# Moving the key tiles' transposes, the gate products, the context shift rows and one pair's modulation in a two-layer diffusion block on one Trainium2 core

## The chip, the core and the metric

The kernel runs on one core of a Trainium2 chip. A core has a matrix engine (TensorE, PE in the profile), a vector engine (DVE), a scalar engine (ACT), a general engine (POOL) and a queue engine (SP) that mostly issues DMAs; each takes its own instructions in order, and semaphores tie them together. The metric is the device time of one execution in microseconds (us), here the median of three runs.

## The reference

Two layers of one backbone, over 1024 latent tokens and 256 context tokens, width 1024. Each layer is an adaLN-modulated, pre-normed mixer with a SiLU gate path and a residual. Layer 0 is grouped-query attention (16 query heads, 4 key heads), layer 1 is multi-head latent attention with compressed keys and values. Cut to what this change touches:

```python
def adaln_params(cond, w_mod, b_mod):
    return jnp.split(jax.nn.silu(cond) @ w_mod + b_mod, 3, axis=-1)      # shift, scale, gate

def kv_heads(kv_a, k_r, n):                                               # layer 1
    kv = (rms_norm(kv_a, p["kv_a_norm"]) @ p["w_kv_b"]).reshape(B, n, 16, 64 + 64)
    k_nope, v = jnp.split(kv, [64], axis=-1)
    return rms_norm(k_nope, p["k_nope_norm"]), rms_norm(k_r, p["k_rope_norm"]), v

def hybrid_layer(x, ctx, c, c_ctx, w_mod, b_mod, norm_w, mixer, ..., with_ctx_out):
    shift, scale, gate = adaln_params(c, w_mod, b_mod)
    shift_c, scale_c, gate_c = adaln_params(c_ctx, w_mod, b_mod)
    h = rms_norm(x, norm_w) * (1.0 + scale[:, None, :]) + shift[:, None, :]
    hc = rms_norm(ctx, norm_w) * (1.0 + scale_c) + shift_c
    y, yc = mixer(h, hc, ...)
    x = x + gate[:, None, :] * y                                          # ctx likewise, in layer 0 only
```

Layer 1's gate row, `silu(c) @ w_mod[:, 2048:] + b`, is needed only where layer 1's output projection is added to x, at the very end.

## The kernel before, in words

Every product of float32 values is made of three matmuls (`mm3`, lines L120, L121, L122): high part by high, high by low, low by high. Weights come by SP into raw buffers `wraw` (pool `rawp`, three buffers), are cast by ACT (`wa`, L184), and their low part is the difference, made by DVE or POOL (`wb`, L163). The stages follow one another: layer 0's projections (0 to 335 us), attention 0 (340 to 703), layer 0's output projection (704 to 831), layer 1's key stage (832 to some 940), its query stage (to 1105), attention 1 (1130 to 1542), layer 1's output projection (to the end).

Attention. A unit is a pair of heads; PE computes scores twice, once for the maxima (`mx`, reduced by DVE at L454 for layer 1 and L495 for layer 0's context units), once for the exponentials (`st`, ACT at L607, result `p`), and then multiplies `p` by v (`av`, `avt`). POOL adds up the `p` of a unit (`acp`, L640); DVE forms the sums (`squares`, `sums`, L705 to L707), and a row of reciprocals goes out and comes back as `rb`; POOL multiplies (`rb`, `os`, L739 and L740) and SP stores to `od`. The maxima become a row of shifts: `do_shift` turns the tile `top` into `turned`, and two DMAs put two rows of it into the tile `shift` (L521) or, for a context unit, `shift_ctx`. In attention 0 units 4, 9, 18 and 19 are context units. Where attention runs (`running`), ACT issues these DMAs, else SP. `Attention.run` takes pairs (t, end) of unit and half; behind a unit's squares it takes the next piece of weight preparation (`extra`, `parts`).

Output projection, `out_proj`. For each of ten tiles of 128 tokens (eight latent, two context): fetch the attention's rows (`oraw`), split them (`oh` by ACT at L870, `ol` by DVE at L871), 48 matmuls `y`, multiply by the gate row `gb` (`yt`, L888), add to `xt` (L889), then call `sink`. In layer 0 `sink0` stores `xt`, norms it (L307), and hands pairs of tiles to `modulate`, where 16 transposes (`tp`, L319) bring the pair into column form, DVE scales it (`hmod`, L323), and the halves `hh`, `hl` are made. A list `hold` delays a pair: `flush(1)` does the oldest pair held.

Key stage of layer 1. `staged(items, *stages)` runs a software pipeline: in step t, stage j is applied to item t - j, and `later` is a stage that does nothing. The stages are `kv_compress` (24 matmuls `mm` of 288 columns, then the norm: `kvms` L1677, `kvrs` by POOL L1680, `kvn` by DVE L1682 and L1683, and a rotary step that ends in L1694, on POOL from the third tile on), `kv_latent` (transposes `tp` of `kvn`, L1701 and L1702, split into `kvh`, `kvl`), `kv_expand` (12 matmuls `mmk` for keys and 12 `mmv` for values, `sq` L1729, `kss` L1731, `kn_ms` L144, `kn` L1714, `v` L1736) and `kv_store` (transposes of `kn`, L1750, `th` and `tl` at L1754 and L1755). DVE keeps the order in which the program writes its work there; PE's order is the scheduler's.

Gate products. `gate_cols(k)` loads 128 rows of w_mod's gate part (tile `wcols`, 512 KB, a `wraw` buffer), and `mod_cols` (L265) has DVE multiply it by the row u and sum: one SCALAR_TENSOR_TENSOR of 128x1024 per k, eight in all. After the eighth, `mod_cols_end` adds the bias (`top`, L271), turns it into a row (`turned`) and SP stores it to `gated`, from which `out_proj` of layer 1 loads `gb`. Here this stands in the key stage:

```python
        with in_order(mybir.EngineType.DVE):
            staged(range(TT), kv_compress, kv_latent, later_with_cols, later, kv_expand, store_all_but_last)
```

## Time and profile before

| | us |
|---|---|
| median of 3 runs | 1639.27 |
| the runs | 1636.88 to 1641.38 |
| the profiled execution's own time | 1638.23 |
| its span, first to last instruction | 1636.3 |
| PE busy | 1596.0 |
| DVE busy | 1150.5 |
| POOL busy | 961.7 |
| ACT busy | 641.2 |
| mean granted clock of PE | 0.995 |

A timeline row reads: start, duration, engine, line, operation, output <- inputs, shapes, count of instructions that the row joins, and in brackets how long the engine sat idle before it and what ended that. PE's matmuls overlap, so a matmul of 512 columns that shows 0.39 us takes a slot of about 0.23. ACTq and SPq are the queues' own instructions, above all the issue of DMAs; they hold the engine's later instructions while they last.

### The profile page before, as it was taken

How to read it: one execution, taken by the hardware profiler on the slowest of the kernel's cores; microseconds unless marked ns; L12 is line 12 of the kernel's file. 1: busy time of each engine (PE TensorE's matmuls, PEld its weight loads, DVE VectorE, ACT ScalarE, POOL GpSimd, SP SyncE). 2: the span in 40 equal slices, each digit the busy share in tenths (PEclk: the TensorE clock that was granted, in tenths of full speed). 3: DMA queues.
4: the chain of work that ended last, by engine and by line, in shares of the span. 5: the costliest groups of instructions: out<-in, count | busy, mean ns of one | idle time of the engine just before them, and what ended most of it. 6: DMA issues, size and time to landing. Idle time of an engine off the chain costs nothing.

```text
span 1636.3 us, 26486 instructions
## 1 busy us (share of the span) xinstructions
PE 1596.0 (98%) x9788; PEld 1178.3 (72%) x9788; DVE 1150.5 (70%) x1951; ACT 641.2 (39%) x943; POOL 961.7 (59%) x629
## 2 busy tenths in 40 slices
PE   7999999999999999999989999999999999999998
PEld 5776788865554555577878798987776767767587
DVE  2674876679998988746576767755778888788231
ACT  3652321235654555522244543341444544435310
POOL 2673640138999999923245555450768878777521
PEclk9999999999999999999999999999999999999999
DMA  8636566742533342274246867768456565562451
GB/s 285 213 106 192 170 196 231 215 134 56 130 82 98 94 108 78 71 224 152 96 138 182 239 200 201 221 202 197 114 137 154 124 149 117 136 145 70 131 179 64
DMA packets 215325, 246.77 MB, mean 151 GB/s; under 512 B 19802, under 2 KB 157266, under 8 KB 215196
## 3 DMA queue, kind: packets, MB, share of 16 engines
q1 hardware_dynamic: 214228, 244.83, 53.7%
q8 instruction: 77, 1.26, 0.3%
q14 instruction: 52, 0.43, 0.1%
q10 hardware_dynamic: 968, 0.25, 0.1%
HBM read 171.23 MB, written 73.63 MB: 150 GB/s over the span
## 4 chain that ended last, share of the span: by engine, by line
PE 84%; DMA 5%; DVE 4%; POOL 2%; ACT 2%; issue 2%; SPq 1%; DVEq 0%; POOLq 0%; ACTq 0%
PE st L600 21%; PE avt L654 9%; PE av L654 9%; PE mm L120 8%; PE mm L122 8%; PE mm L121 8%; PE mx L452 4%; PE y L120 3%; PE y L121 3%; PE y L122 3%; PE mx L486 2%; DVE wb L163 1%; DMA q1l<-tl 1%; PE mx L462 1%; DMA mraw<-in_l_w_mod 1%
## 5 line engine op out<-in xcount | busy, mean ns | idle before, releaser
L640 POOL TENSOR_TENSOR acp<-acp,p 128x1024 f32<-128x1024 f32 x188 | 448.6, 2386 | 12.6
L607 ACT ACTIVATE p<-st 128x1024 f32<-128x1024 f32 x328 | 336.3, 1027 | 154.5 <-PE st L600 145.7
L454 DVE TENSOR_REDUCE m<-mx 128x1 f32<-128x512 f32 x256 | 175.8, 691 | 66.2 <-PE mx L452 60.3
L640 POOL TENSOR_TENSOR acp<-p 128x1024 f32<-128x1024 f32 x34 | 81.5, 2398 | 191.7 <-ACT p L607 191.7
L495 DVE TENSOR_REDUCE m<-mx 128x1 f32<-128x1024 f32 x128 | 150.2, 1219 | 39.4 <-PE mx L486 38.9
L654 PE MATMUL avt<-p,v 128*64 128x512 f32 x672 | 149.3, 596 | 0.7 <-ACT p L607 0.6
L654 PE MATMUL av<-p,v 128*64 128x512 f32 x640 | 141.1, 595 | 0.0
L163 POOL TENSOR_TENSOR wb<-wraw,wa 128x512 fp32r<-128x512 f32 (+3 forms) x65 | 91.0, 1415 | 80.4 <-ACT wa L184 80.4
L120 PE MATMUL mm<-wa,hh 128*128 128x512 f32 (+2 forms) x336 | 126.1, 375 | 1.7 <-ACT hh L1041 1.1
L600 PE MATMUL st<-QH,KH 64*128 64x512 f32 x320 | 122.5, 407 | 0.6 <-DVE gth L354 0.5
L122 PE MATMUL mm<-wa,hl 128*128 128x512 f32 (+2 forms) x336 | 121.5, 362 | 1.6 <-DVE hl L1044 1.6
L121 PE MATMUL mm<-wb,hh 128*128 128x512 f32 (+2 forms) x336 | 121.1, 360 | 0.0
L600 PE MATMUL st<-QH,KL 64*128 64x512 f32 x320 | 117.9, 391 | 0.0
L600 PE MATMUL st<-QL,KH 64*128 64x512 f32 x320 | 117.6, 390 | 0.0
L654 PEld LDWEIGHTS avt<-p,v 128*64 128x64 f32 x672 | 46.0, 137 | 93.8 <-issue 82.9
L654 PEld LDWEIGHTS av<-p,v 128*64 128x64 f32 x640 | 44.3, 137 | 87.9 <-issue 87.3
L120 PE MATMUL mm<-hh,wa 128*128 128x512 f32 (+1 forms) x264 | 103.0, 390 | 0.9 <-ACT th L102 0.9
L120 PE MATMUL y<-wa,oh 128*128 128x512 f32 (+1 forms) x268 | 103.3, 386 | 0.0
L122 PE MATMUL y<-wa,ol 128*128 128x512 f32 (+1 forms) x268 | 102.8, 384 | 0.0
L121 PE MATMUL y<-wb,oh 128*128 128x512 f32 (+1 forms) x268 | 102.8, 384 | 0.0
L122 PE MATMUL mm<-hh,wb 128*128 128x512 f32 (+1 forms) x264 | 101.3, 384 | 0.0
L121 PE MATMUL mm<-hl,wa 128*128 128x512 f32 (+1 forms) x264 | 101.3, 384 | 0.0
(267 smaller groups left out, 4045.1 us busy)
## 6 DMA issues: line engine op xcount, KB each, us to landing
wraw<-in_l_w_in SPq DMA_DIRECT2D x28, 512.0 KB
wcols<-in_l_w_mod_t SPq DMA_DIRECT2D x24, 512.0 KB
KH<-k1h SPq DMA_DIRECT2D x32, 320.0 KB
KL<-k1l SPq DMA_DIRECT2D x32, 320.0 KB
rb<-rrow SPq DMA_DIRECT2D x72, 128.0 KB
mraw<-in_l_w_mod SPq DMA_DIRECT2D x16, 512.0 KB
wraw<-in_l_w_out SPq DMA_DIRECT2D x16, 512.0 KB
QA<-q0h SPq DMA_DIRECT2D x32, 256.0 KB
```

Of the source, the lines that this page charges most:

```text
L120: pe.matmul(ps, lhsT=lh(k), rhs=rh(k), start=first and i == 0, stop=False)
L121: pe.matmul(ps, lhsT=lh(k), rhs=rl(k), start=False, stop=False)
L122: pe.matmul(ps, lhsT=ll(k), rhs=rh(k), start=False, stop=last and i == len(ks) - 1)
L163: eng.tensor_sub(lo, a, b)
L452: pe.matmul(held["m"][:, cs], lhsT=q[:, t * P:(t + 1) * P], rhs=k[:, ks], start=j == 0, stop=j == len(pairs) - 1)
L454: dve.reduce_max(s["m"][:, i, n:n + 1], held["m"], axis=AX.X)
L486: pe.matmul(m[:, n * 512:n * 512 + 512], lhsT=q[:, i * P:(i + 1) * P], rhs=k[:, n * 512:n * 512 + 512], start=True, stop=True)
L495: dve.reduce_max(s["m"][:, i, 0:1], m, axis=AX.X)
L600: pe.matmul(ps[:, n * 512:(n + 1) * 512], lhsT=lh, rhs=rh, start=j == 0, stop=j == last)
L607: act.activation(p, ps, AF.Exp, scale=self.ops["scale"])
L640: pool.tensor_add(t, a, b)
L654: pe.matmul(s["av"][64 * n:64 * n + 64, :], lhsT=s["v"][:, kt, u["vc"]:u["vc"] + 64], rhs=p[:, n * 512:(n + 1) * 512], start=kt == kts[0], ...
```

## The change

Four things, independent of each other.

First, `sink0` calls `flush(1)` for tile 3 and no longer for tile 2. The first pair's modulation so comes behind the products of tile 3, the fourth tile; the later pairs stay where they are. Second, the context units' two shift DMAs are issued by SP also while attention runs. Third, in the key stage one `later` moves ahead of `kv_latent`: a tile's transposes are made two steps behind its products, and its expansion at the step at which it was. Fourth, the gate products leave the key stage. Attention gets a table `beside` that maps (unit, half) to a function; it loads the first two pieces at unit 10, does one product each at units 11, 12 and 13, two at 14, and three and the end of the row at (15, 0). The row u is loaded there, and piece k + 2 is fetched behind product k.

```diff
--- before.py
+++ after.py
@@ -373,6 +373,7 @@
             self.started = 0
             self.done = 0
             self.todo = []
+            self.beside = {}
             self.last_lat = [u for u in units if u["kind"] == "lat"][-1]
 
         def open_early(self, st):
@@ -518,7 +519,7 @@
                 r = turned[at_:at_ + 32, :]
                 turn_squares(r, raw(m))
                 for n in range(2):
-                    (act if self.running else sp).dma_start(raw(s["crow"][n]), r[4 * n:4 * n + 4, :])
+                    (act if self.running and u["kind"] == "lat" else sp).dma_start(raw(s["crow"][n]), r[4 * n:4 * n + 4, :])
 
             self.turns.append((self.units.index(u), turn))
 
@@ -815,6 +816,7 @@
                             if late:
                                 self.add_up(u, [], [])
                             self.squares(u, p2s[n1 // 2:])
+                        self.beside.get((t, int(end)), lambda: None)()
                         if t % 2 and end:
                             if parts:
                                 parts()
@@ -1619,9 +1621,9 @@
                 sp.dma_start(x1d[tt * P:(tt + 1) * P, :], xt)
             norm_rows(xt, small)
             xs_of.setdefault(tt // 2, []).append(xt)
-            if tt % 2 == 0:
+            if tt % 2 == 0 and tt != 2 or tt == 3:
                 flush(1)
-            else:
+            if tt % 2:
                 hold.append((tt // 2, xs_of[tt // 2]))
 
         def started0():
@@ -1758,26 +1760,11 @@
 
         kept = []
 
-        u = st.enter_context(tc.tile_pool(name="urow1", bufs=1, **right)).tile([P, D], F32, name="u0", tag="u0")
-        sp.dma_start(u, ud[0:1, :].broadcast_to([P, D]))
-
-        def gate_cols(k):
-            w = rawp.tile([P, D], F32, name="wcols", tag="wraw")
-            sp.dma_start(w, ins["l1_w_mod_t"][2 * D + k * P:2 * D + (k + 1) * P, :])
-            mod_cols(w, u.unsqueeze(1), w, 2, k, (0,))
-            if k == KT - 1:
-                mod_cols_end(2)
-
         def store_all_but_last(tt, held):
             kept.append(held) if tt == TT - 1 else kv_store(tt, held)
 
-        def later_with_cols(tt, kv):
-            if tt < KT:
-                gate_cols(tt)
-            return kv
-
         with in_order(mybir.EngineType.DVE):
-            staged(range(TT), kv_compress, kv_latent, later_with_cols, later, kv_expand, store_all_but_last)
+            staged(range(TT), kv_compress, later, kv_latent, later, kv_expand, store_all_but_last)
         wqa = load_weight(w_in1, KT, 288, 384)
         with tc.manual_schedule(engines={mybir.EngineType.PE, mybir.EngineType.DVE}):
             early[0] = proj1(0, wqa, 384)
@@ -2018,6 +2005,26 @@
     stL, stLP = ExitStack(), ExitStack()
     at.open_late(stL, stLP)
     first = []
+    u = stE.enter_context(tc.tile_pool(name="urow1", bufs=1, **right)).tile([P, D], F32, name="u0", tag="u0")
+    sp.dma_start(u, ud[0:1, :].broadcast_to([P, D]))
+    cols = {}
+
+    def gate_fetch(k):
+        cols[k] = rawp.tile([P, D], F32, name="wcols", tag="wraw")
+        sp.dma_start(cols[k], ins["l1_w_mod_t"][2 * D + k * P:2 * D + (k + 1) * P, :])
+
+    def gate_cols(n):
+        for _ in range(n):
+            k = cols.pop("next", 0)
+            mod_cols(cols[k], u.unsqueeze(1), cols[k], 2, k, (0,))
+            cols["next"] = k + 1
+            if k + 2 < KT:
+                gate_fetch(k + 2)
+            if k == KT - 1:
+                mod_cols_end(2)
+
+    at.beside = {(10, 1): lambda: [gate_fetch(k) for k in range(2)], (11, 1): lambda: gate_cols(1), (12, 1): lambda: gate_cols(1),
+                 (13, 1): lambda: gate_cols(1), (14, 1): lambda: gate_cols(2), (15, 0): lambda: gate_cols(3)}
     at.run(24, 2, pieces, lambda: first.extend(fetch_first(1, 3)))
     stLP.close()
     stE.close()
```

Line numbers of the new kernel are one or two higher from `do_shift` on (L521 is L522, L675 is L676, L1701 is L1703, L871 is L873), and 13 lower behind the key stage.

PE in layer 0's output projection, at the first pair's transposes. The names carry buffer numbers: y_7343 is the second half of tile 2, xt_7162 and xt_7167 are tiles 0 and 1. Before:

```order
L120 MATMUL y_7343<-wa_3339,oh_7339 128x512
L121 MATMUL y_7343<-wb_3340,oh_7339 128x512
L122 MATMUL y_7343<-wa_3339,ol_7340 128x512
L319 MATMUL tp_7410<-ident_72,xt_7162 128x128
L319 MATMUL tp_7410<-ident_72,xt_7167 128x128
```

The same transposes in the new kernel, where y_7414 is the second half of tile 3:

```order
L120 MATMUL y_7414<-wa_3339,oh_7410 128x512
L121 MATMUL y_7414<-wb_3340,oh_7410 128x512
L122 MATMUL y_7414<-wa_3339,ol_7411 128x512
L319 MATMUL tp_7483<-ident_72,xt_7162 128x128
L319 MATMUL tp_7483<-ident_72,xt_7167 128x128
```

The transposes moved behind 48 more products; the second pair's follow after the 48 of tile 4.

DVE at the same place, before (L307 norms a tile, L323 scales the transposed pair, L888 and L889 are the sum of the next tile):

```order
L307 TENSOR_SCALAR xt<-xt,x_rs 128x1024
L144 TENSOR_SCALAR x_ms<-xss 128x1
L888 TENSOR_TENSOR yt<-y,gb 128x512
L307 TENSOR_SCALAR xt<-xt,x_rs 128x1024
L888 TENSOR_TENSOR yt<-y,gb 128x512
L323 TENSOR_SCALAR hmod<-tp,A_114,B_116 128x256
L889 TENSOR_TENSOR xt<-xt,yt 128x512
L323 TENSOR_SCALAR hmod<-tp,A_114,B_116 128x256 x3
L144 TENSOR_SCALAR x_ms<-xss 128x1
L323 TENSOR_SCALAR hmod<-tp,A_114,B_116 128x256 x2
```

And in the new kernel:

```order
L307 TENSOR_SCALAR xt<-xt,x_rs 128x1024
L144 TENSOR_SCALAR x_ms<-xss 128x1
L890 TENSOR_TENSOR yt<-y,gb 128x512
L307 TENSOR_SCALAR xt<-xt,x_rs 128x1024
L890 TENSOR_TENSOR yt<-y,gb 128x512
L891 TENSOR_TENSOR xt<-xt,yt 128x512
L873 TENSOR_TENSOR ol<-oraw,oh 128x1024
L144 TENSOR_SCALAR x_ms<-xss 128x1
L307 TENSOR_SCALAR xt<-xt,x_rs 128x1024
L890 TENSOR_TENSOR yt<-y,gb 128x512 x2
L323 TENSOR_SCALAR hmod<-tp,A_114,B_116 128x256
L891 TENSOR_TENSOR xt<-xt,yt 128x512
```

DVE's first work on the pair moved behind tile 3's split and sum.

PE at the head of the key stage, from the first tile's expansion on, before:

```order
L120 MATMUL mmk<-wa,kvh 128x512
L121 MATMUL mmk<-wb,kvh 128x512
L1702 MATMUL tp<-ident,kvn 32x128
L122 MATMUL mmk<-wa,kvl 128x512
L120 MATMUL mmk<-wa,kvh 128x512
L121 MATMUL mmk<-wb,kvh 128x512
L122 MATMUL mmk<-wa,kvl 128x512
L1701 MATMUL tp<-ident,kvn 128x128 x2
L120 MATMUL mmv<-wa,kvh 128x512
L121 MATMUL mmv<-wb,kvh 128x512
L1702 MATMUL tp<-ident,kvn 32x128
L122 MATMUL mmv<-wa,kvl 128x512
```

And in the new kernel:

```order
L120 MATMUL mmk<-wa,kvh 128x512
L121 MATMUL mmk<-wb,kvh 128x512
L1704 MATMUL tp<-ident,kvn 32x128
L1703 MATMUL tp<-ident,kvn 128x128 x2
L120 MATMUL mmv<-wa,kvh 128x512
L121 MATMUL mmv<-wb,kvh 128x512
L1704 MATMUL tp<-ident,kvn 32x128
L122 MATMUL mmk<-wa,kvl 128x512
L120 MATMUL mmk<-wa,kvh 128x512
L121 MATMUL mmk<-wb,kvh 128x512
L122 MATMUL mmk<-wa,kvl 128x512
L122 MATMUL mmv<-wa,kvl 128x512
```

The transposes of the third tile (the second L1701 row's place) stand behind two products here and behind six before, and a fourth tile's, which stood among the products further on, come a step later.

DVE at the tail of the key stage, before:

```order
L103 TENSOR_TENSOR krl<-tp,krh 32x128
L265 SCALAR_TENSOR_TENSOR wcols,cols_71<-wcols,u_8241 128x1024
L163 TENSOR_TENSOR wb<-wraw,wa 128x384
L271 TENSOR_TENSOR top_84<-cols_71,colsT 128x8
L95 STREAM_TRANSPOSE turned<-top_84 32x32 x4
L1731 TENSOR_REDUCE kss<-sq 128x8
L144 TENSOR_SCALAR kn_ms<-kss 128x8
L1731 TENSOR_REDUCE kss<-sq 128x8
L144 TENSOR_SCALAR kn_ms<-kss 128x8
L1714 TENSOR_TENSOR kn<-mmk,kn_rs 128x512 x2
```

And in the new kernel:

```order
L103 TENSOR_TENSOR krl<-tp,krh 32x128
L1733 TENSOR_REDUCE kss<-sq 128x8
L163 TENSOR_TENSOR wb<-wraw,wa 128x384
L144 TENSOR_SCALAR kn_ms<-kss 128x8
L163 TENSOR_TENSOR wb<-wraw,wa 128x384
L1733 TENSOR_REDUCE kss<-sq 128x8
L144 TENSOR_SCALAR kn_ms<-kss 128x8
L1716 TENSOR_TENSOR kn<-mmk,kn_rs 128x512 x2
```

The last gate product, the sum `top` and its turn are gone from between `krl` and `kss`, and three weight parts `wb` stand elsewhere.

DVE at the end of attention 1, before:

```order
L707 RECIPROCAL turned<-turned 32x32
L99 TENSOR_REDUCE squares<-p 128x64
L99 TENSOR_REDUCE squares<-acp 128x32
L95 STREAM_TRANSPOSE sums<-squares 32x96 x4
L705 TENSOR_REDUCE turned<-sums 32x32
L706 TENSOR_REDUCE turned<-turned 32x32
L707 RECIPROCAL turned<-turned 32x32
L871 TENSOR_TENSOR ol<-oraw,oh 128x896 x3
```

And in the new kernel:

```order
L708 RECIPROCAL turned<-turned 32x32
L99 TENSOR_REDUCE squares<-p 128x64
L265 SCALAR_TENSOR_TENSOR wcols,cols_71<-wcols,u_11903 128x1024 x2
L99 TENSOR_REDUCE squares<-acp 128x32
L95 STREAM_TRANSPOSE sums<-squares 32x96 x4
L706 TENSOR_REDUCE turned<-sums 32x32
L707 TENSOR_REDUCE turned<-turned 32x32
L708 RECIPROCAL turned<-turned 32x32
L265 SCALAR_TENSOR_TENSOR wcols,cols_71<-wcols,u_11903 128x1024 x3
L271 TENSOR_TENSOR top_84<-cols_71,colsT 128x8
L95 STREAM_TRANSPOSE turned<-top_84 32x32 x4
L873 TENSOR_TENSOR ol<-oraw,oh 128x896 x3
```

Two products stand ahead of the last squares but one, and three products with the row's end between the last reciprocal and layer 1's first `ol`.

## The prediction

> **What bounds the kernel now.** I read the page's busy times first, then the chain of waits of TensorE (PE), then the timeline around each wait that the change touches, then the other engines' timelines there.
>
> ```profile
> PE 1596.0 (98%) x9788; PEld 1178.3 (72%) x9788; DVE 1150.5 (70%) x1951; ACT 641.2 (39%) x943; POOL 961.7 (59%) x629
> ```
>
> PE is busy for 1596.0 of 1636.3 us, and the change neither adds nor removes a matmul. What it can win lies in the 40 us of idle PE time, and in time at a lower clock. The view of waits (engine, line waited for: us in total, times, longest) lists that idle time; four of its rows belong to places that the change touches.
>
> ```profile
> PE tp L1701 <- DVE kvn L1682: 3.7, 3, 1.3
> ...
> PE mmk L120 <- DVE kn L1714: 2.3, 2, 1.5
> PE tp L319 <- DVE xt L307: 2.2, 1, 2.2
> ...
> PE mx L486 <- DVE m L495: 1.9, 2, 1.4
> ```
>
> **Part 1: the first pair's transposes behind tile four.** In layer 0's output projection the 16 transposes L319 of tiles 0 and 1 stand right behind the products y of tile 2. Timeline of PE, then DVE, then windows (busy time of PE, its weight load, DVE, ACT, POOL; third from the right is the granted PE clock), then PE at a later pair:
>
> ```profile
> 736.66 0.39 PE L122 MATMUL y<-wa,ol 128*128 128x512 f32 x1
> 737.34 0.30 PE L319 MATMUL tp<-ident,xt 128*128 128x128 f32 x1 [0.29 <-DVE x_ms L144]
> 739.80 2.81 PE L319 MATMUL tp<-ident,xt 128*128 128x128 f32 x15 [2.16 <-DVE xt L307]
> ...
> 744.27 0.39 PE L122 MATMUL y<-wa,ol 128*128 128x512 f32 x1
> ```
> ```profile
> 738.44 1.30 DVE L307 TENSOR_SCALAR xt<-xt,x_rs 128x1024 f32<-128x1024 f32 x1 [0.58 <-DMA x1d<-xt]
> ```
> ```profile
> 742.00:743.00 1.00, 1.00 (x5) 0.90 (x4) 1.00 (x4) 1.00 (x3) 0.00 (x0) 0.50 0.00 0
> ...
> 766.00:777.00 11.00, 11.00 (x54) 9.20 (x53) 8.98 (x15) 3.43 (x6) 4.81 (x4) 1.00 0.56 183
> 777.00:788.00 11.00, 11.00 (x50) 9.11 (x49) 4.12 (x6) 2.21 (x3) 1.84 (x2) 1.00 0.28 89
> ```
> ```profile
> 812.03 1.91 PE L319 MATMUL tp<-ident,xt 128*128 128x128 f32 x16
> 813.70 0.48 PE L120 MATMUL y<-wa,oh 128*128 128x512 f32 x1
> ```
>
> The second row stops because tile 1 is normed only at 738.44 to 739.74. Behind the wait of 2.16 us the clock is 0.50. From the slot after the last y (736.66 + 0.23 = 736.89) to the start of the sixth y of tile 3 (744.27) go 7.38 us. A later pair needs 813.70 - 812.03 = 1.67 us for its 16 transposes, and the first five y need about 0.31 + 4 x 0.23 = 1.22: 2.89. So 4.5 us are lost here, 2.45 of them waits and 2.0 the low clock. With tile 3's products (48 x 0.23 = 10.9 us) ahead of the transposes, both tiles have been normed for some 8 us when PE gets there. I take the whole 4.5. What is late next: pair 1 follows one tile later instead of two, so DVE gets two heavy tiles in a row. The windows of 11 us show DVE at 8.98 in a tile with a pair and 4.12 in one without; 8.98 twice still fits. Bounds: 2.5 (the low clock comes anyway) to 4.5.
>
> The Trainium skill, "TensorE: Matmul & The Clock Gate", part on HAM oscillation, says that PE idle for more than about 3.4 us brings the half rate. The idle time here is 2.45 us in all, and the half clock came nonetheless; read literally, the page would not lay it to this wait, and the sum would be 2.0 smaller. I go by the trace.
>
> **Part 2: context rows by SyncE (SP).** The context unit's two shift DMAs leave ACT's queue. ACT, DVE and PE in attention 0, at the second context unit:
>
> ```profile
> 495.83 0.58 ACTq L521 DMA_DIRECT2D shift<-turned  x1
> 496.98 2.38 ACTq L521 DMA_DIRECT2D shift_ctx<-turned  x2
> 499.40 1.14 ACT L184 CAST wa<-wraw 128x512 fp32r<-128x512 f32 x2 [8.68 <-DMA sg<-sgd]
> 500.45 0.58 ACT L675 COPY os<-avt 128x512 f32<-128x512 f32 x1
> ```
> ```profile
> 500.57 1.86 DVE L163 TENSOR_TENSOR wb<-wraw,wa 128x512 fp32r<-128x512 f32 x1 [2.41 <-ACT wa L184]
> ```
> ```profile
> 501.08 0.50 PE L600 MATMUL st<-QA,KA 64*128 64x512 f32 x2 [1.08 <-ACT os L675]
> ...
> 503.62 0.50 PE L486 MATMUL mx<-KA,QA 64*128 64x512 f32 x2 [1.35 <-DVE m L495]
> ```
>
> ACT cannot cast wa before its two issues are through at 499.36; os follows, PE waits 1.08 for it, and wb, held up by wa, keeps DVE from the maxima, for which PE waits 1.35. Without the two, wa starts right behind the lane shift (about 496.5), three us earlier, and both waits close: 2.4 us. On SP the two issues (2.4 us there too at worst) stand between loads of QA and QL for a later unit, which hides them. At the other context units nothing waits for ACT: nothing. Bounds: 0 (the lane shift's own wait, until 495.83, sets it) to 2.4; I take 2.4, since ACT's rows join without a gap.
>
> **Part 3: key tiles two steps behind.** Head of the key stage, PE, then POOL and DVE:
>
> ```profile
> 849.78 0.41 PE L1701 MATMUL tp<-ident,kvn 128*128 128x128 f32 x2 [1.19 <-DVE kvn L1682]
> ...
> 852.02 0.28 PE L1702 MATMUL tp<-ident,kvn 128*32 128x128 f32 x1 [1.37 <-POOL kvn L1694]
> ...
> 853.91 0.50 PE L120 MATMUL mmk<-wa,kvh 128*128 128x512 f32 x1 [0.68 <-ACT v L1736]
> ...
> 857.98 0.40 PE L120 MATMUL mm<-wa,hh 128*128 128x288 f32 x1 [0.68 <-ACT v L1736]
> ...
> 863.89 0.47 PE L120 MATMUL mmv<-wa,kvh 128*128 128x512 f32 x1 [0.76 <-ACT sq L1729]
> ```
> ```profile
> 850.56 1.41 POOL L1694 TENSOR_TENSOR kvn<-krt,krt 128x32 f32<-128x32 f32 x1
> ```
> ```profile
> 850.65 1.20 DVE L265 SCALAR_TENSOR_TENSOR wcols<-wcols,u 128x1024 f32<-128x1024 f32 x1
> ```
>
> The first two of the three waits for kvn (3.7 - 1.19 = 2.5 us) stay: the order of PE is the same up to there. The five waits shown sum to 4.68. The third tile's transposes are still early (in the new order only two products stand before them, so they wait again, about 1.2). The wait for POOL falls from 1.37 to about 0.5, since the gate product beside which L1694 took 1.41 is gone; the two for the copies of v stay; the last (0.76) goes, since the fourth tile's transposes now come a whole step later. That is 0.9 + 0.8 and some 0.3 for matmuls that restart less often: 2.0. Bounds: 0 (the waits only move) to 4.7.
>
> **Part 4: gate products at the attention's end.** Two places. Where they leave, the tail of the key stage (PE; DVE; POOL; ahead of it the two waits for kn L1714, 2.3 us):
>
> ```profile
> 911.96 0.50 PE L120 MATMUL mmv<-wa,kvh 128*128 128x512 f32 x1 [0.99 <-ACT v L1736]
> ```
> ```profile
> 907.53 1.84 DVE L265 SCALAR_TENSOR_TENSOR wcols<-wcols,u 128x1024 f32<-128x1024 f32 x1
> ...
> 909.96 0.86 DVE L95 STREAM_TRANSPOSE turned<-top 32x32 f32<-32x32 f32 x4
> ```
> ```profile
> 905.91 2.38 POOL L163 TENSOR_TENSOR wb<-wraw,wa 128x384 fp32r<-128x384 f32 x2
> ```
>
> The last product (1.84) and the turn of the row (0.86) stand on DVE ahead of the sums that kn waits for, and eight loads of 512 KB stand ahead of the next weights. 1.84 + 0.86 = 2.7 us earlier on DVE against 0.99 + 2.3 = 3.3 of waits: I take 2.5, bounds 1 to 3.3. In between, the stage is bound by PE, and seven products that leave there give nothing.
>
> Where they arrive, units 11 to 15 of attention 1. DVE, POOL, SP and PE:
>
> ```profile
> 1496.38 1.39 DVE L454 TENSOR_REDUCE m<-mx 128x1 f32<-128x512 f32 x2 [2.02 <-PE mx L452]
> ...
> 1523.46 0.35 DVE L707 RECIPROCAL turned<-turned 32x32 f32<-32x32 f32 x1
> 1540.35 3.77 DVE L871 TENSOR_TENSOR ol<-oraw,oh 128x896 fp32r<-128x896 f32 x3 [16.54 <-ACT oh L870]
> ```
> ```profile
> 1484.83 9.73 POOL L640 TENSOR_TENSOR acp<-acp,p 128x1024 f32<-128x1024 f32 x4
> ...
> 1528.86 9.72 POOL L640 TENSOR_TENSOR acp<-acp,p 128x1024 f32<-128x1024 f32 x4
> ```
> ```profile
> 1532.04 1.75 SPq L839 DMA_DIRECT2D oraw<-od  x3
> ```
> ```profile
> 1544.24 0.50 PE L108 MATMUL y<-wa,oh 128*128 128x512 f32 x1
> ```
>
> One product of 1.20 us falls into DVE's gap of 2.02 before a unit's maxima, when POOL's adds are over (1484.83 + 9.73 = 1494.56): free. Once the last unit's maxima are taken nothing of PE waits for DVE, and behind the last reciprocal (1523.81) it idles 16.54 us, long enough for the last three and the row's turn. But the 1.84 shows what POOL does to such a product: POOL's wb ends at 908.29, 0.76 after the product was due, and 1.20 + 0.76 = 1.96 is close to 1.84. Beside the adds from 1528.86 on (2.43 each) three products and three adds alternate: the products end not three times 1.20 after about 1524 but near 1535, the store of the gated row follows at about 1536, and on SP the loads of oraw, which stood at 1532.04, come behind it, near 1539. The 12.2 us from that issue to the first y at 1544.24 hold a landing, a cast on ACT and the split ol (3.77 for three, 1.26 for one); with 7 of them gone, 5.2 are left, about what these need, so the first y may wait about 1 us. POOL's last adds end some 3.7 us later, which lies within the bounds. I take a loss of 0.8; bounds 0 to 4. The eight fetches go on SP behind the next units' keys, and all but the last land a unit before their product; SP's queue waits for nothing else there that PE sees, so I cost them at nothing.
>
> The Trainium skill, "SBUF — State Buffer", section "SBUF: two separate sides", calls the ports shared by VectorE and GpSimd an exclusive lock for a whole instruction, also where VectorE has two inputs in SBUF. The rows 1.84 and 1.41 agree. Without such a lock, Part 4's loss would be 0.
>
> **Sum.** 4.5 + 2.4 + 2.0 + 2.5 - 0.8 = 10.6 us. The profiled execution took 1638.23 (span 1636.3 and 1.9 around it), so it would take 1627.6. It stood 1.04 below the median of the three runs, 1639.27; against that median 1628.7.
>
> **Rivals.**
> First, the key stage's waits only move (parts 3 and 4 give 0.5 in place of 4.5): 1632.7. For it: the copies of v and the third tile stay late. Against: DVE has 8 x 1.20 + 0.86 = 10.5 us less work there. 0.17.
> Second, the pair behind tile four brings its own wait: DVE at 8.98 of 11 for two tiles running, or the low clock was not the wait's doing. It costs 2 to 3: 1631.2, or 1630.7 where only the 2.0 of the clock stay. For it: the clock was 0.50 behind a mere 2.45 us of idle time. Against: DVE stays under 11, and the clock was 1.00 at the later pair, which did not wait. 0.13. The case of 1630.7 is also what the Trainium skill's page "TensorE: Matmul & The Clock Gate" (HAM oscillation) would give.
> Third, the rows' move does nothing, because ACT is held by the wait of the lane shift or SP puts the loads off: 1631.1. 0.12.
> Fourth, on the other side: DVE gets no turn between POOL's adds until POOL pauses, at 1538.58 or, with the unit's two multiplications, about 1541 (my estimate). Then three products and the turn (3.6 + 0.86) take until 1543 to 1546, and the gated store holds SP until then; oraw comes as now some 3 us later, and the first y another 8 to 12.2 behind it: at 1554 to 1561, 10 to 17 late. About 14 us lost where 11.4 are won: 1641.9. It decides from a gated store later than about 1544. Against: at 907.53 DVE did get its turn between two wb of POOL. 0.05, half of it beyond 0.3%.
> The forecast itself, all parts near their price: 0.50; the rest (0.03) is a shift of the query stage's waits by 3 us either way.
>
> **How the numbers follow.** Predicted 1628.7. Each of the first three rivals alone stays under 1634.4 (0.3%, 4.9 us, is about what a measurement of this kernel can tell from no change). Two together, or the fourth, do not. Faster 0.88, same 0.09, slower 0.03. The range: downward all parts at their upper ends, 4.5 + 2.4 + 4.7 + 3.3 = 14.9 and some 2 of the runs' spread: 1622.0; upward the first rival with one other: 1635.0.
>
> **What the changed profile would show.** Right: no wait at the first L319, PEclk 1.00 there; no wait for os and m at the second context unit; the wait for POOL's kvn under 0.6, none for kn behind 0.5; the gated store before 1540 on the old clock of times, and first y waiting under 1.5. Wrong: a new wait of y on DVE's yt around the second pair, kvn waits summing to over 5 in the key stage, or a wait over 3 ahead of layer 1's first y.

## The result and the profile after

The changed kernel takes 1622.95 us, median of 4 runs (1622.35 to 1624.84); the kernel before, run beside it, 1638.3 (1636.88 to 1641.38). The ratio is 0.9906, 95% interval 0.9890 to 0.9921: 15.4 us faster, where 10.6 were forecast. The time lies in the stated range, near its lower end. The profiled execution took 1622.44, its span is 1620.6.

The page's busy times after:

```profile
PE 1587.7 (98%) x9788; PEld 1181.1 (73%) x9788; DVE 1160.3 (72%) x1951; ACT 641.3 (40%) x943; POOL 961.3 (59%) x629
```

PE is busy for 8.3 us less with the same 9788 matmuls, so not all of the gain is idle time: part of it is matmuls that ran at half clock before and do not now, as windows below show. The view of waits after:

```profile
PE tp L1703 <- DVE kvn L1684: 3.7, 3, 1.3
...
PE tp L1942 <- DVE tl L103: 2.0, 1, 2.0
...
PE y L108 <- ACT oh L872: 1.8, 2, 1.2
PE mx L487 <- DVE m L496: 1.6, 2, 1.0
...
PE mmv L120 <- ACT v L1738: 1.1, 1, 1.1
...
PE tp L1704 <- POOL kvn L1696: 0.2, 1, 0.2
```

Gone are the waits at L319, for os, for kn, and the early ones for v and sq; the wait for POOL's kvn fell from 1.4 to 0.2. Left are the wait for the maxima (1.9 before, 1.6 now) and kvn's 3.7. New is 1.2 for oh ahead of layer 1's first y. Between the same instructions of the two traces:

| place | before | after | gained |
|---|---|---|---|
| start to the context unit's wait (503.62, 500.09) | 503.62 | 500.09 | 3.5 |
| to layer 1's first `tp` of kvn (838.16, 830.27) | 334.54 | 330.18 | 4.4 |
| key stage, to the last `tp` of kn (943.60, 927.74) | 105.44 | 97.47 | 8.0 |
| query stage and attention 1, to layer 1's first y (1544.24, 1528.60) | 600.64 | 600.86 | -0.2 |
| to the end of the span | 92.06 | 92.00 | 0.1 |

These rows, key stage before and then after, carry the third line. I call the stage up to the first `tp` of kn its head, and the rest its tail. The first `tp` of kn is 30.39 us behind the first `tp` of kvn before and 25.16 after, so 5.2 of the 8.0 are won at the head.

```profile
868.55 0.82 PE L1750 MATMUL tp<-ident,kn 128*128 128x128 f32 x6
...
943.60 1.03 PE L1750 MATMUL tp<-ident,kn 128*128 128x128 f32 x8
```
```profile
830.27 0.44 PE L1703 MATMUL tp<-ident,kvn 128*128 128x128 f32 x2 [1.32 <-DVE kvn L1684]
...
840.60 0.44 PE L1703 MATMUL tp<-ident,kvn 128*128 128x128 f32 x2 [1.14 <-DVE kvn L1684]
...
855.43 1.03 PE L1752 MATMUL tp<-ident,kn 128*128 128x128 f32 x8
...
927.74 1.03 PE L1752 MATMUL tp<-ident,kn 128*128 128x128 f32 x8
```

The first line of the table is not the change alone. Windows of the first 30 us, before and then after (third number from the right: PE's granted clock), show half rate in the one and none in the other, though nothing was changed there:

```profile
25.00:30.00 5.00, 4.38 (x29) 3.32 (x30) 2.43 (x6) 3.06 (x6) 2.30 (x2) 0.71 1.04 332
```
```profile
25.00:30.00 5.00, 4.38 (x37) 3.30 (x36) 2.88 (x6) 3.05 (x6) 2.35 (x2) 1.00 1.08 350
```

By the last wait of layer 0's projections the new trace is 2.1 us ahead (171.96 and 169.82), so that the context unit gives the other 1.4. And in the query stage the same wait of 2.0 us (999.38 before, 983.50 after) was followed by a low clock before and by the full one after:

```profile
998.00:1003.00 5.00, 3.62 (x14) 3.65 (x15) 4.63 (x14) 1.84 (x4) 2.03 (x4) 0.69 1.11 361
```
```profile
982.00:987.00 5.00, 3.50 (x21) 3.50 (x22) 3.75 (x10) 1.73 (x4) 1.73 (x3) 1.00 1.09 359
```

From the last `tp` of kn to the `mx` of attention 1 that waits for QH (1108.89 before, 1091.71 after) the query stage is 1.3 us shorter; from there to layer 1's first y attention 1 is 1.5 longer (435.35 and 436.89), so that the fourth line of the table is nearly 0. The clock is taken up behind the experiments.

### The profile page after: what moved, and what is told of

The parts are those of the page before. It is cut to its first block, busy times and chain, and to the rows that moved or that the text cites. A ratio compares the mean times of both kernels' runs of the same rounds, so it can differ in the third digit from the quotient of the medians.

```text
span 1620.6 us, 26473 instructions
## 1 busy us (share of the span) xinstructions
PE 1587.7 (98%) x9788; PEld 1181.1 (73%) x9788; DVE 1160.3 (72%) x1951; ACT 641.3 (40%) x943; POOL 961.3 (59%) x629
## 4 chain that ended last, share of the span: by engine, by line
PE 84%; DVE 6%; DMA 3%; POOL 2%; issue 2%; ACT 1%; SPq 1%; ACTq 0%; DVEq 0%; POOLq 0%
PE st L601 19%; PE avt L655 8%; PE mm L120 8%; PE mm L122 8%; PE mm L121 8%; PE av L655 8%; PE mx L453 4%; PE y L120 4%; PE y L122 4%; PE y L121 4%; PE mx L487 2%; DVE wb L163 1%; DVE squares L99 1%; PE mx L463 1%; DVE wcols L265 1%
```

## The experiments

**One part at a time.** Each of the four parts alone on the kernel before, run beside it (26 runs, median 1638.26).

The pair behind tile four:

```diff
-            if tt % 2 == 0:
+            if tt % 2 == 0 and tt != 2 or tt == 3:
                 flush(1)
-            else:
+            if tt % 2:
                 hold.append((tt // 2, xs_of[tt // 2]))
```

> The kernel before with only the first pair's transposes moved behind tile four. Theory (the wait of 2.45 us and the half clock behind it, 2.0 us, both go): 4.3 us faster, about 1634.0 against 1638.3, first L319 without a wait. Rival (the half clock is a matter of when the wait falls and would not have come in most executions): 2.4 us faster, about 1635.9. In the trace the key stage and the query stage stay as in the kernel before: waits of 7.9 us at the key stage's head, 3.3 at its tail.

Measured: 1631.82, ratio 0.9962 (0.9949 to 0.9975), 6.4 us faster. From layer 0's first y to layer 1's first `tp` of kvn, here and then in the kernel before:

```profile
703.91 0.50 PE L108 MATMUL y<-wa,oh 128*128 128x512 f32 x1 [0.57 <-ACT oh L870]
...
833.42 0.44 PE L1701 MATMUL tp<-ident,kvn 128*128 128x128 f32 x2 [1.32 <-DVE kvn L1682]
```
```profile
704.09 0.50 PE L108 MATMUL y<-wa,oh 128*128 128x512 f32 x1 [0.57 <-ACT oh L870]
...
838.16 0.44 PE L1701 MATMUL tp<-ident,kvn 128*128 128x128 f32 x2 [1.31 <-DVE kvn L1682]
```

That is 129.51 us against 134.07: 4.6 us, and no row of the waits names L319. The theory holds for the place. The rest of the 6.4 lies elsewhere and fits the clock: its mean over the runs is 0.9978 against 0.9958, and 0.0020 of 1636 us is 3.3 us, of which the half clock behind L319 has 1.7 by its windows in the kernel before.

The shift rows on SP:

```diff
-                    (act if self.running else sp).dma_start(raw(s["crow"][n]), r[4 * n:4 * n + 4, :])
+                    (act if self.running and u["kind"] == "lat" else sp).dma_start(raw(s["crow"][n]), r[4 * n:4 * n + 4, :])
```

> The kernel before with only the context units' shift rows on SP. Theory (as in the changed kernel's trace: the wait for os goes, the one for m stays at about 1.0 because wb on DVE is held by POOL's adds): 1.4 us faster, about 1636.9, wb near 2.6 us long. Rival (the forecast's: both waits go): 2.4 us faster, about 1635.9. On the clock: if the half rate depends only on a wait's length, it shows behind the L319 wait of 2.2 us and behind the query stage's wait of 2.0 us as in the kernel before; if on when the wait falls, it is missing behind one of them, since everything behind 500 us comes 1.4 us earlier.

Measured: 1636.72, ratio 0.9995 (0.9978 to 1.0011): too small for the time to show. The trace shows the place: no wait for os, 0.8 for m. Why the second wait stays is seen in the changed kernel, ACT, DVE, PE:

```profile
492.99 1.14 ACT L184 CAST wa<-wraw 128x512 fp32r<-128x512 f32 x2 [4.16 <-DVE sums L95]
```
```profile
496.24 2.66 DVE L163 TENSOR_TENSOR wb<-wraw,wa 128x512 fp32r<-128x512 f32 x1
```
```profile
500.09 0.49 PE L487 MATMUL mx<-KA,QA 64*128 64x512 f32 x2 [1.04 <-DVE m L496]
```

wa now is done at 494, wb starts as soon as DVE is free, but takes 2.66 us where it took 1.86; it ends at 498.90 and the maxima start then. In the trace of the part alone the low clock showed behind both the L319 wait and the query stage's, although both came 3.7 us earlier than in the kernel before.

The key tiles' transposes two steps behind, the gate products kept in the key stage. The stage `later_with_cols` moves one place back as well, so that each product comes one tile later in DVE's order than in the kernel before:

```diff
-            staged(range(TT), kv_compress, kv_latent, later_with_cols, later, kv_expand, store_all_but_last)
+            staged(range(TT), kv_compress, later, kv_latent, later_with_cols, kv_expand, store_all_but_last)
```

> The kernel before with only the key tiles' transposes two steps behind their products; the gate products stay in the key stage. Theory (the delay itself takes away the two waits for v and the 0.76, and shortens the wait for POOL's kvn): the stage's head is 3 to 4 us shorter, its tail is as before, about 1634.8. Rival (the head's gain comes from the gate products that left DVE): at most 1 us, about 1637.5.

Measured: 1633.85, ratio 0.9975 (0.9960 to 0.9989), 4.4 us faster. The head is 3.6 us shorter (first `tp` of kvn to first `tp` of kn, 835.64 to 862.39, 26.75 against 30.39), as the theory had it. But it is not the delay alone that does this: the first product stands behind the fourth tile's kvn, where the kernel before has it behind the third's, and two products instead of three stand ahead of the first kss. How much of the 3.6 is the delay's own is not shown.

```profile
847.94 0.48 DVE L1682 SCALAR_TENSOR_TENSOR kvn<-mm,kvrs,bc_l_kv_a_norm 128x256 f32<-128x256 f32 x1 [0.82 <-POOL kvrs L1680]
...
849.44 1.20 DVE L265 SCALAR_TENSOR_TENSOR wcols<-wcols,u 128x1024 f32<-128x1024 f32 x1
```

The tail is 2.4 longer, against the theory: the first row is the wait there, the second the window around it, with two stretches of half clock.

```profile
916.44 0.79 PE L120 MATMUL mmk<-wa,kvh 128*128 128x512 f32 x1 [3.10 <-DVE kn L1714]
```
```profile
914.00:922.00 8.00, 5.56 (x14) 4.29 (x15) 5.85 (x13) 2.15 (x5) 5.02 (x4) 0.61 0.81 224
```

The whole stage gains 1.2 in this trace (104.25 against 105.44). The two stretches cost 3.4 us of it, by windows of 1 us; without them it would have gained some 4.6 by my estimate, close to the 4.4 of the medians, whose mean clocks are equal (0.9957 and 0.9958). The last product is nearer to the stage's end as well: 30.2 us ahead of the last `tp` of kn, where it was 36.1.

The gate products moved, the transposes one step behind as before; the edit is the diff's parts on `beside` and `gate_cols`, with

```diff
-            staged(range(TT), kv_compress, kv_latent, later_with_cols, later, kv_expand, store_all_but_last)
+            staged(range(TT), kv_compress, kv_latent, later, later, kv_expand, store_all_but_last)
```

> The kernel before with only the gate products moved to the attention's end; the transposes stay one step behind. Theory (the products cost the key stage 1.1 us at its head, through POOL's kvn at L1694, and 2.8 at its tail, and their new place costs 1.5): 2.4 us faster, about 1635.9; L1694 takes 0.25 us at 850 where it took 1.41; a wait of about 1.2 before layer 1's first y. Rival (the products carry most of the key stage's gain of 8.0): 6 us faster, about 1632.

Measured: 1627.92, ratio 0.9946 (0.9924 to 0.9968), 10.3 us faster. The theory falls, the rival is nearer. The key stage's first `tp` of kvn, first and last `tp` of kn:

```profile
836.89 0.44 PE L1703 MATMUL tp<-ident,kvn 128*128 128x128 f32 x2 [1.32 <-DVE kvn L1684]
...
863.48 1.03 PE L1752 MATMUL tp<-ident,kn 128*128 128x128 f32 x8
...
934.47 1.03 PE L1752 MATMUL tp<-ident,kn 128*128 128x128 f32 x8
```

It takes 97.58 us: 7.9 gained, 3.8 of it at the head. The wait ahead of layer 1's first y is 1.19, as the theory had it. The mean clock is 0.9970 against 0.9958, which is some 2 of the 10.3 us.

**Without part 3.** The changed kernel with the transposes one step behind again.

```diff
-            staged(range(TT), kv_compress, later, kv_latent, later, kv_expand, store_all_but_last)
+            staged(range(TT), kv_compress, kv_latent, later, later, kv_expand, store_all_but_last)
```

> The changed kernel with the transposes again one step behind their products (part 3 undone, the rest kept). Theory (with the gate products gone the delay has nothing left to take away: parts 3 and 4 of the forecast removed the same waits, since part 4 alone gained 7.9 us in the key stage by the trace and both together 8.0): same time as the changed kernel, 1623 within 1 us, no wait for v at the stage's head. Rival (the delay gives 2.0 of its own, as forecast): 1625, with waits for v or for kvn that the changed kernel has not.

Measured: 1621.97, ratio to the kernel before 0.9904 (0.9881 to 0.9926), where the changed kernel has 0.9906. Its key stage:

```profile
855.88 1.03 PE L1752 MATMUL tp<-ident,kn 128*128 128x128 f32 x8
...
926.86 1.03 PE L1752 MATMUL tp<-ident,kn 128*128 128x128 f32 x8
```

From 829.28, its first `tp` of kvn, that is 26.60 and 97.58: the head is 1.4 longer than in the changed kernel, the tail as much shorter. Part 3 gives nothing once the gate products are gone.

**How the products cost the head 3.8 us.** The kernel before with each product replaced, in its place, by a row sum of the same tile, which reads one operand instead of two.

```diff
-            mod_cols(w, u.unsqueeze(1), w, 2, k, (0,))
+            dve.reduce_sum(sums_of[2][:, k, 0:1], w, axis=AX.X)
```

> The kernel before with each gate product, still in the key stage, replaced by a row sum of the same tile with one operand (1.2 us as well); the gate row is then not the reference's. If the lock between VectorE and POOL is what the products cost there: POOL's L1694 takes 0.25 us instead of 1.41 and the stage's head gains about as much as with the products gone, 3 to 4 us. If it is their place in VectorE's order, ahead of the next tile's norm: L1694 takes 0.25, one wait of 1.37 falls to about 0.2, but kvn comes every 3.6 us as before (2.5 with the products gone) and the waits for v stay: a gain of 1 to 1.5 at the head.

There is one run (1636.85, within the spread of the kernel before), so only its trace is used. The head takes 29.45 us (836.94 to 866.39): 0.9 gained of the 3.8. Groups of POOL in the key stage, first of this kernel, then of the kernel before:

```profile
L1694 POOL TENSOR_TENSOR kvn<-krt,krt 128x32 f32<-128x32 f32 x6 | 1.5, 252 | 0.5
```
```profile
L1694 POOL TENSOR_TENSOR kvn<-krt,krt 128x32 f32<-128x32 f32 x6 | 6.2, 1028 | 0.5
```

So with two operands the product holds up POOL, and with one it does not. But kvn comes as slowly as before (849.15 and 852.80 there, 3.65 apart). DVE's rows for two tiles in this kernel, and in the one whose products are gone:

```profile
847.91 0.48 DVE L1682 SCALAR_TENSOR_TENSOR kvn<-mm,kvrs,bc_l_kv_a_norm 128x256 f32<-128x256 f32 x1 [0.81 <-POOL kvrs L1680]
...
849.42 1.20 DVE L1767 TENSOR_REDUCE cols<-wcols 128x1 f32<-128x1024 f32 x1
...
851.55 0.48 DVE L1682 SCALAR_TENSOR_TENSOR kvn<-mm,kvrs,bc_l_kv_a_norm 128x256 f32<-128x256 f32 x1 [0.82 <-POOL kvrs L1680]
```
```profile
847.87 0.48 DVE L1684 SCALAR_TENSOR_TENSOR kvn<-mm,kvrs,bc_l_kv_a_norm 128x256 f32<-128x256 f32 x1 [0.81 <-POOL kvrs L1682]
...
850.38 0.48 DVE L1684 SCALAR_TENSOR_TENSOR kvn<-mm,kvrs,bc_l_kv_a_norm 128x256 f32<-128x256 f32 x1 [0.82 <-POOL kvrs L1682]
```

3.64 us against 2.51, the difference being the instruction of 1.20 that stands ahead of the next tile's kvms. At the head each tile's norm is a loop through DVE, POOL and DVE again, and every DVE instruction in its order lengthens the loop. That is 2.9 of the 3.8; the other 0.9 is POOL held up. The two waits for v stay too (0.67 each), and with the products gone they are gone. ACT does not cause them: it copies v as soon as PE's products are there, as this row of the kernel before says.

```profile
853.27 0.59 ACT L1736 COPY v<-mmv 128x512 f32<-128x512 f32 x1 [0.56 <-PE mmv L122]
```

**The other place: the attention's end.** The changed kernel there, DVE, POOL, SP, PE:

```profile
1499.50 1.95 DVE L265 SCALAR_TENSOR_TENSOR wcols<-wcols,u 128x1024 f32<-128x1024 f32 x1
...
1501.38 3.38 DVE L265 SCALAR_TENSOR_TENSOR wcols<-wcols,u 128x1024 f32<-128x1024 f32 x1
...
1514.90 2.20 DVE L271 TENSOR_TENSOR top<-cols,colsT 128x8 f32<-128x8 f32 x1
```
```profile
1513.74 10.71 POOL L641 TENSOR_TENSOR acp<-acp,p 128x1024 f32<-128x1024 f32 x4
```
```profile
1518.03 0.30 SPq L274 DMA_DIRECT2D gated<-turned  x1
...
1523.25 1.80 SPq L841 DMA_DIRECT2D oraw<-od  x3
```
```profile
1528.60 0.50 PE L108 MATMUL y<-wa,oh 128*128 128x512 f32 x1 [1.24 <-ACT oh L872]
```

Products of 1.2 us take up to 3.38, and even the sum `top` over eight columns takes 2.20. The gated store at 1518.03 holds SP, the loads of oraw follow at 1523.25, and the first y waits 1.24. The same products as row sums of one operand:

```diff
-            mod_cols(cols[k], u.unsqueeze(1), cols[k], 2, k, (0,))
+            dve.reduce_sum(sums_of[2][:, k, 0:1], cols[k], axis=AX.X)
```

> The changed kernel with each gate product replaced by a row sum of the same tile, which reads one operand of 128x1024 where the product reads two; the gate row is then not the reference's. Theory (VectorE with two operands in SBUF and POOL lock each other out): all eight take 1.2 us also beside POOL's adds, POOL's adds stay at 2.4, and the first y waits under 0.4. Rival (any read of SBUF by VectorE beside POOL is slowed, or the queue's order does it): the last five still take 1.8 to 3.4.

```profile
1505.79 3.47 DVE L2019 TENSOR_REDUCE cols<-wcols 128x1 f32<-128x1024 f32 x3
```
```profile
1510.94 9.73 POOL L641 TENSOR_TENSOR acp<-acp,p 128x1024 f32<-128x1024 f32 x4
```

Three take 3.47 together, POOL's four adds 9.73 as in the kernel before (9.72), and no wait over 0.3 stands ahead of y; the one run took 1620.26. It is not the reading beside POOL that costs. The row sum also writes one column where the product writes 1024; that this is not the reason shows in `top`, which reads two operands and writes eight columns, and which took 2.20 beside POOL's adds and 0.17 in the next kernel below, where POOL had stood idle for 4 us. The second operand is what is left. The Trainium skill, "SBUF — State Buffer", section "SBUF: two separate sides", says that VectorE (DVE) with two inputs in SBUF, the core's working memory, and a GpSimd (POOL) operation that reads SBUF exclude each other for a whole instruction; these two runs agree, by 1.2 against 1.8 to 3.4 us.

**Other places for the products.** One each at units 6 to 13, the row's end at (15, 0):

```diff
-            if k == KT - 1:
-                mod_cols_end(2)
-
-    at.beside = {(10, 1): lambda: [gate_fetch(k) for k in range(2)], (11, 1): lambda: gate_cols(1), (12, 1): lambda: gate_cols(1),
-                 (13, 1): lambda: gate_cols(1), (14, 1): lambda: gate_cols(2), (15, 0): lambda: gate_cols(3)}
+
+    at.beside = {(5, 1): lambda: [gate_fetch(k) for k in range(2)], (15, 0): lambda: mod_cols_end(2)}
+    for t in range(6, 14):
+        at.beside[t, 1] = lambda: gate_cols(1)
```

> The changed kernel with the eight gate products one each at units 6 to 13, behind the unit's squares, where POOL pauses, and only the row's end at (15, 0). Theory (the end lost 1.5 us because five products and the sum waited for POOL's adds and POOL for them): no product longer than 1.4 us, no wait for oh ahead of layer 1's first y, 1.2 to 1.5 us faster than the changed kernel, about 1621.5. Rival (the wait for oh comes from the gated store's place on SP, or the products cost PE their maxima at the earlier units): the wait stays at 1 or waits for m come up, 1623 or more.

Measured: 1624.57 (1621.10 to 1628.20), no faster. The wait for oh is gone. But the first six products took 2.0 to 3.1 us, and a fetch held SP from 1326 to 1335, until POOL's weight part freed a raw buffer; queries queued behind it (SP, POOL, PE):

```profile
1335.15 0.36 SPq L2014 DMA_DIRECT2D wcols<-in_l_w_mod_t  x1
```
```profile
1332.58 2.54 POOL L163 TENSOR_TENSOR wb<-wraw,wa 128x512 fp32r<-128x512 f32 x2
```

PE then waited 1.16 for QH at 1345.94 and 0.54 at 1397.86. Two each at units 11 to 13, one at 14, one at (15, 0):

```diff
-    at.beside = {(10, 1): lambda: [gate_fetch(k) for k in range(2)], (11, 1): lambda: gate_cols(1), (12, 1): lambda: gate_cols(1),
-                 (13, 1): lambda: gate_cols(1), (14, 1): lambda: gate_cols(2), (15, 0): lambda: gate_cols(3)}
+    at.beside = {(10, 1): lambda: [gate_fetch(k) for k in range(2)], (11, 1): lambda: gate_cols(2), (12, 1): lambda: gate_cols(2),
+                 (13, 1): lambda: gate_cols(2), (14, 1): lambda: gate_cols(1), (15, 0): lambda: gate_cols(1)}
```

> The changed kernel with the gate products two each at units 11, 12 and 13, in POOL's pause behind the unit's adds, one at 14 and one at (15, 0). Theory (the end's loss is products and POOL's adds locking each other out; where POOL pauses they are free, and no weight part waits for a raw buffer there): no wait for oh ahead of layer 1's first y, at most 0.5 for maxima, 1.2 us faster than the changed kernel. Rival (two products a unit push the maxima back: 2.5 us of work in a gap of 2.0): a wait for m or mx of 0.5 to 1 in each of three units, no gain.

Measured: 1623.16 (1620.68 to 1624.34), no faster. The wait for oh is gone, but at unit 12 POOL ran late and the two products met its adds:

```profile
1453.20 3.41 DVE L265 SCALAR_TENSOR_TENSOR wcols<-wcols,u 128x1024 f32<-128x1024 f32 x1
```
```profile
1457.27 0.57 PE L453 MATMUL mx<-KH,QH 64*128 64x512 f32 x1 [1.85 <-DVE m L455]
```

The rival was right there, with half clock behind the wait. Starting one unit earlier, one each at units 10 to 13, two at 14, two at (15, 0):

```diff
-    at.beside = {(10, 1): lambda: [gate_fetch(k) for k in range(2)], (11, 1): lambda: gate_cols(1), (12, 1): lambda: gate_cols(1),
-                 (13, 1): lambda: gate_cols(1), (14, 1): lambda: gate_cols(2), (15, 0): lambda: gate_cols(3)}
+    at.beside = {(9, 1): lambda: [gate_fetch(k) for k in range(2)], (10, 1): lambda: gate_cols(1), (11, 1): lambda: gate_cols(1),
+                 (12, 1): lambda: gate_cols(1), (13, 1): lambda: gate_cols(1), (14, 1): lambda: gate_cols(2), (15, 0): lambda: gate_cols(2)}
```

> The changed kernel with the gate products started one unit earlier, so that two instead of three are left for (15, 0): one each at units 10 to 13, two at 14, two at (15, 0). Theory (each of the last products costs about 2.3 us beside POOL's adds, and SP's loads of oraw have 5.5 us of slack of which the changed kernel uses 6.8): the gated store comes 2.3 us earlier, no wait for oh above 0.3, no wait for maxima, 1.2 us faster than the changed kernel, about 1621.7. Rival (the product at unit 10 meets POOL's adds or holds a raw buffer that SP's loads of keys wait behind): a wait for QH or m of 1 to 2 at unit 10 to 12, 1623 or more.

Measured: 1618.55 (1618.18 to 1619.35), ratio to the kernel before 0.9887 (0.9871 to 0.9904), the fastest of all; the changed kernel's interval, 0.9890 to 0.9921, overlaps it. The gated store comes 4.5 us sooner behind the `mx` of attention 1 that waits for QH than in the changed kernel (1512.76 - 1090.90 = 421.86 against 1518.03 - 1091.71 = 426.32): one product of 2.3 less, 1.11 for `top` instead of 2.20, and 1.1 that stands there already at the first product of unit 14 (406.65 against 407.79) and has no row of its own. The first y follows without a wait, and attention 1 up to it is 2.5 shorter (434.42 against 436.89), of which the wait has 1.24 and that 1.1 most of the rest. The clock helped as well: 0.9998 over the runs against 0.9990, some 1.3 us. The store and the first y:

```profile
1512.76 0.27 SPq L274 DMA_DIRECT2D gated<-turned  x1
```
```profile
1525.32 0.50 PE L108 MATMUL y<-wa,oh 128*128 128x512 f32 x1
```

**What was left of part 2.** The changed kernel with the low parts of that weight half made by POOL alone, and then with the products moved as in the second of the three kernels above as well:

```diff
-    wo.append(load_weight(ins["l0_w_out"], KT, 512, 512, 2, todo=pieces))
+    wo.append(load_weight(ins["l0_w_out"], KT, 512, 512, 0, todo=pieces))
```

> The changed kernel with the low parts wb of layer 0's second half of output weights made by POOL alone; four of them were DVE's, 1.8 to 2.7 us each where a lone one takes 0.7. Theory (what was left of part 2's gain, a wait of 1.04 for the maxima and one of 0.58, stands on wb waiting for POOL's adds): both waits gone, 1.6 us faster than the changed kernel. Rival (POOL is full there and its adds come late instead): the waits turn into waits for p or acp, no gain.

> The changed kernel with both: gate products two each at units 11 to 13, one at 14, one at (15, 0), and wb of layer 0's second half of output weights by POOL alone. If both theories hold, 2.8 us faster than the changed kernel, about 1620; if only one holds, 1621 to 1622.

Measured: 1623.55 (ratio 0.9911, 0.9893 to 0.9929) and 1627.52 (0.9933, 0.9916 to 0.9950), neither faster than the changed kernel. The waits for the maxima of attention 0 are gone in both, though the second has one of 1.6 in attention 1, as in the kernel with two products each at units 11 to 13. Others came earlier in attention 0; PE in the first of the two:

```profile
456.84 0.50 PE L601 MATMUL st<-shift,minus 64*128 64x512 f32 x1 [0.81 <-DMA shift<-turned]
...
488.98 0.49 PE L487 MATMUL mx<-KA,QA 64*128 64x512 f32 x1 [1.18 <-DMA QA<-q0h]
```

POOL is busy there for 111 of the 120 us from 400 to 520, as the rival feared, but what came late were a load and shift rows and not p or acp; that POOL made them late is not shown. The two gains did not add up. Most of what the second kernel lacks against the changed one, 4.6 us, is clock: 0.9967 against 0.9990, some 3.8.

## Why the prediction was right, and where it was off

**Part 1: 4.5 forecast, 4.6 alone and 4.3 in the changed kernel.** Right, the low clock included, of which the windows show 1.7 where 2.0 were taken. DVE with two heavy tiles in a row made nobody wait.

**Part 2: 2.4 forecast, 1.4 found.** The step that failed is "both waits close". wb was held not only by wa but by DVE's own `squares`, behind which it started at 496.24, and then by POOL's adds, which ran from 491.08 to 501.13: it took 2.66 instead of 1.86. The wait for os closed; that for m went from 1.35 to 1.04.

**Parts 3 and 4 in the key stage: 2.0 + 2.5 forecast, 8.0 found.** The bound of part 3 and that of part 4 together allowed it, the values taken did not. Two steps were mis-sized. Part 4's sum counted only the tail and called the products in between free, since the stage is bound by PE there; but the head is not bound by PE, and there part 4 alone gives 3.8, by the DVE order (2.9) and POOL's L1694 (0.9). Only the second was in the sum, and under part 3. Its tail gives 4.1 alone, over the bound of 3.3, which was made of the waits shown and left out what each costs around them: ahead of the wait of 0.99 the last matmul's slot ends at 910.81 (910.58 + 0.23), 1.15 before 911.96, and the next start follows after 0.34 instead of 0.23, some 0.27 more in all. And "the two for the copies of v stay" was wrong: they, and the one for sq, stay with one operand and go with the products, so the slow kvn had made three waits, and POOL held up the fourth. Part 3, on the other hand, gives nothing on top of part 4; alone, with the products one tile later, it gave 3.6 at the head, of which its own share is not shown.

**Part 4 at the attention's end: 0.8 lost forecast, 1.5 found**, 1.24 of it the wait for oh; the store's place on SP and the nearly free products at units 11 to 13 (1.32 to 1.48 us) came as told. The last three alternated with POOL as forecast, but with an add and the two multiplications ahead of its last four adds. That the row's end waits as well (2.20 for `top`) was not seen.

**The clock.** The four places give 4.4 + 1.4 + 8.0 - 1.5 = 12.3 of the 15.7 us between the spans. The other 3.4 lie at the start (2.1) and in the query stage (1.3), where the trace before loses 3.4 and 1.7 us to half clock and the new one none. No term of the sum had these, so this share of the gain is luck as far as the forecast goes. It is not only luck of one trace: 51 runs of the kernel before, beside these experiments, have a mean clock of 0.9960 and a mean span of 1635.9, the changed kernel's four 0.9990 and 1621.3. Within the 51, runs at 0.998 have 1632.6 on average and those at 0.994 1639.3, 1.66 us for each 0.001. So 0.0030 more clock is, by my estimate, about 5 of the 14.6 us between the means and fewer and shorter waits about 10. The forecast had 2.0 of the clock, at L319 alone. Which of the changed places brings the rest can't be told from four runs.

The rivals: the second and the fourth did not come, and the third came by half, but by another mechanism. The first, that the key stage's waits only move, did not come either: parts 3 and 4 do overlap, but what overlaps is the gain, and the whole was larger than forecast.

## What to carry to other kernels

Before pricing work that leaves an engine, look whether the stage around it runs a loop through that engine's order: there every instruction costs its whole duration, however idle the engine looks. Two parts of a change that remove the same waits must be priced alone and together. And an instruction of DVE with two operands in SBUF belongs where POOL pauses; count on its own time plus up to one POOL instruction where it does not.

## What the runs showed of the hardware

The half rate of PE's clock does not follow from a wait's length alone. In one trace of each of the 14 kernels, the wait of 2.01 to 2.03 us in the query stage, which all of them have, was followed by half clock in 8 and by the full clock in 6. Behind the 2.45 to 3.85 us at L319 it came in all five kernels that have that wait, and in the first 35 us, where waits of 0.9 to 2 us stand, in 4 of 14. A stretch costs about 1.7 us (3.4 us at half rate). The Trainium skill, "TensorE: Matmul & The Clock Gate", Part 1, calls the window free-running; that one wait is or isn't followed by half clock agrees with it. Its limit of about 3.4 us of idle time does not hold here: 2.0 us were enough in 8 of the 14 kernels.

DVE's two-operand instructions beside POOL were lengthened by up to nearly one whole add of POOL (2.4 us): 3.38 us for 1.2, and 2.20 for a sum over eight columns.
